# Branch B's first projection chunk among the attention fillers, and a three-piece end for the last tile's normalization

## The chip, the core and the metric

One core of a Trainium2 chip runs the kernel. Its engines each work through a queue of their own: TensorE (PE in the profile, its weight loads PEld), VectorE (DVE), ScalarE (ACT), GpSimd (POOL), and SyncE (SP), which issues the DMAs here. The metric is the device time of one execution in microseconds, lower is better; a kernel is executed several times and the median is given.

## What is computed

A single encoder layer on x of 1024 tokens by 1024 channels, float32:

```python
h = x @ w_in[l]
qa, ka, va, qb, kb, vb, ga, gb = jnp.split(h, split_pts, axis=-1)
y_a = chunk_band_attention(heads_a(qa), heads_a(ka), heads_a(va), rel_bias[l]) @ w_proj_a[l]
y_b = stick_breaking_attention(heads_b(qb), heads_b(kb), heads_b(vb)) @ w_proj_b[l]
gate_a = jax.nn.sigmoid(ga + b_gate[l, :D])
gate_b = jax.nn.sigmoid(gb + b_gate[l, D:])
mix = (gate_a * y_a + gate_b * y_b) @ w_out[l]
x = layer_norm(DEEPNORM_ALPHA * x + mix, ln1_g[l], ln1_b[l])
...
x = layer_norm(DEEPNORM_ALPHA * x + ffn, ln2_g[l], ln2_b[l])
```

There are 8 heads of width 64 in each branch. Branch A is softmax attention over a band with a bias by distance; branch B weights keys by a product of sigmoids over the keys between. The feed-forward block between the two normalizations is a gated one with 2816 hidden channels.

## The kernel before

**Numbers.** Every float32 operand is split into a high and a low part, and a product is three matmuls (high by high, high by low, low by high) into one accumulator in PSUM. A matmul is 128 by 128 weights against up to 512 columns.

**Stages.** The input projection comes first (to about 333 us of the span), with seven products for eight. Then attention (333 to 638 us), then branch B's projection with its gates (638 to 682 us), the output projection and the first normalization, and the feed-forward block, whose last part adds four hidden blocks to each of eight row tiles, normalizes the tile and stores it.

**Attention and its fillers.** The loop over `vsteps` (from L1021) takes 16 heads in turn, branch A's eight first, each in 12 steps. `hidx` is the head and `pos` the step in it. A step issues some score blocks ahead of need (`wunits`, as many as `LEAD` says), one group of transposes (`turn`) and, two steps late, the products with v (`mult`). A score block gives work to DVE, ScalarE and GpSimd, and the transposes wait for it. To fill PE in the meantime there is a generator, `fill_all` (L871), of independent matmuls of 512 columns: six gate chunks of 48 matmuls (tile `gps`), then branch A's projection, eight chunks of 24 (tile `yAps`), 480 in all. `goal` counts how many should have been issued; `fill_until(t)` issues up to `t`. `FILL[hidx]` is added to `goal` over a head's 12 steps, `AHEAD = 8` at the very start, and a few steps move it by hand: head 7, the last of branch A, is given 2 at step 3 and 4 at step 4, so that PE has something to do while the next branch starts. Whatever is left is issued after the last step.

**Order.** The framework that builds the program sorts instructions by their place in the text and by when they should be ready; what `tc.keep_in_program_order` names keeps its order. `turn(tied)` names its first transpose so. Each engine then runs its own queue in order, and an instruction that waits holds up those behind it.

**Buffers.** Tiles are taken from rings of buffers by tag (`SLOTS`, and `BANKS` for PSUM: two accumulators each of "mm" and "sc", three of "tr", one of "pv"). A new tile waits until the old one in its buffer has no user left. Fillers use "mm", scores use "sc", transposes "tr".

**Branch B's projection** (the loop at L1128) goes over eight chunks of 128 output channels in the order 6, 7, 5, 4, 2, 3, 1, 0. Each has two halves of 512 tokens, and a half is four operand tiles `yh[4 + k]`, `yl[4 + k]` (one for each pair of heads) times three matmuls: 12. Half 0 accumulates in an "sc" bank, half 1 in an "mm" bank (tile `yBps`). DVE multiplies each by the gate (L1146) and adds branch A's part (L1147); then the sums for the output projection follow, on ScalarE and DVE. The weights of two chunks come as one pair of tiles, `begin_proj(1, cc)`, the first of them at step 4 of the last head. After chunk 6 the weights of the output projection are split (`end_21()`, tile `wl_o` at L552).

**The last tile.** `layer_norm` (L1177) gathers statistics on DVE, raises the variance to a power on GpSimd, and then DVE does `(t - mean) * g`. With `quick` set, DVE also does `t * scale + b`, for each piece in `cuts` (L1190), and `done` stores the piece. Without it, ScalarE scales the whole tile (L1194) and GpSimd adds b (L1195). Of the eight tiles at the end only the last has `quick`, with two pieces of 512.

Of the kernel before, what the change touches and what calls it, by code (L numbers as in the profile page):

```python
# [13 lines left out]
AF = mybir.ActivationFunctionType  # L14
ALU = mybir.AluOpType
# [3 lines left out]
P = 128  # L19
S = 1024  # L20
D = 1024
# [9 lines left out]
HW = 512  # L31
LO, HI = slice(0, HW), slice(HW, 2 * HW)
# [3 lines left out]
LAG = 2  # L36
LEAD = ((6, 8, 9, 9, 10, 10, 11, 11, 12, 12, 13, 13), (7, 8, 9, 9, 10, 10, 11, 11, 12, 12, 13, 14))

FILL = (18, 18, 18, 18, 18, 18, 18, 34, 39, 39, 38, 38, 39, 37, 38, 38)
AHEAD = 8  # L40


# [6 lines left out]
def hybrid_trunk_kernel(ctx: ExitStack, tc, x, xt, w_first, w_v, w_in, b_gate, rel_bias, w_proj,  # L49
# [6 lines left out]
    nc = tc.nc  # L56
# [19 lines left out]
    def bank(tag, name):  # L76
        return ps.tile([P, HW], F32, tag=tag, name=name, bufs=BANKS[tag])
# [4 lines left out]
    mm = nc.tensor.matmul  # L82
# [208 lines left out]
    for j in range(4):  # L291
        cs = (LO, HI)[j % 2]
# [578 lines left out]
    def fill_all():  # L871
# [23 lines left out]
        for cc in range(4):  # L895
# [29 lines left out]
            if cc < 3:  # L925
                w = got.pop()

    def begin_proj(br, cc):

        hl = [slot("op", f"wy{p}{br}_{cc}", F32R) for p in "hl"]  # L930
        for d, t in zip(wp_dr[4 * br + cc], hl):
            dma(t.bitcast(F32), d)
        return lambda: hl
# [87 lines left out]
    for si, (hd, g, st, box) in enumerate(vsteps):  # L1021
        hidx, pos = si // nhead, si % nhead
        if hidx < 14 and pos == 8:
            load_qk(heads[hidx + 2])
            if hidx < 6:
                later.append([3, heads[hidx + 2]["end_bias"]])
        if pos == 4:
            if hidx < 15:
                load_v(heads[hidx + 1])
            else:  # L1030
                next_w = begin_proj(1, 3)()
                end_11, end_21 = (begin_wo(name, raws, "xt")
                                  for name, raws in (("11", ("qs", "kh")), ("21", ("kl", "v"))))
        if hidx == 15 and pos == 10:
            end_11()
        early = hd["br"] == 0 and st == LAG - 1 and len(pend) == LAG
        if early and g == 1:
            pend.pop(0)()
        if hidx == 7 and pos in (3, 4):
            if pos == 4:  # L1040
                fill_until(goal + 2)
            goal += pos - 1 + pos // 4
        elif hd["br"] == 0 and pos in (3, 5):
            goal += 4 - pos
        if hd["br"] == 0 and pos == 2:
            fill_until(goal + 0.5)
        tied = False
        while wi < min(hidx * 8 + LEAD[hd["br"]][pos], len(wunits)):
            wunits[wi]()
            wi += 1  # L1050
            tied = hd["br"] == 1
        if hidx == 7 and pos == 4:
            tied = True
            fill_until(goal)
        elif tied:
            fill_until(goal + 1)
        if si == 0:
            goal += AHEAD
            heads[1]["end_bias"](False)
            fill_until(goal)  # L1060
        if st == 0:
            steps_of[(hidx, g)] = value_steps(hd, g, box)
        turn, mult = steps_of[(hidx, g)][st]
        for item in list(later):
            item[0] -= 1
            if item[0] == 0:
                later.remove(item)
                item[1]()
        turn(tied)
        last = goal  # L1070
        goal += FILL[hidx] / nhead
        fill_until(0.5 * (last + goal))
        if early and g == 0:
            pend.pop(0)()
        pend.append(mult)
        wait = hd["br"] == 0 and st == LAG
        while len(pend) > LAG + wait:
            pend.pop(0)()
        fill_until(goal)
# [48 lines left out]
    for n, c in enumerate((6, 7, 5, 4, 2, 3, 1, 0)):  # L1128
# [7 lines left out]
        if c in kept:  # L1136
            mA = kept[c]
        else:
            mA = slot("op", f"mA{c}")
            dma(mA, m_dr[c])  # L1140
        for hf, cs in enumerate((LO, HI)):
            acc = bank(("sc", "mm")[hf], f"yBps{c}_{hf}")
            mm3(acc, [(w[0][:, ks], w[1][:, ks], yh[4 + k][:, cs], yl[4 + k][:, cs])
                      for k, ks in ((k, slice((c % 2) * HW + k * P, (c % 2) * HW + (k + 1) * P))
                                    for k in range(4))])
            nc.vector.tensor_tensor(gB[:, cs], acc, gB[:, cs], ALU.mult)  # L1146
            nc.vector.tensor_tensor(mA[:, cs], gB[:, cs], mA[:, cs], ALU.add)  # L1147
        m_raw[c] = mA
# [28 lines left out]
    def layer_norm(t, g, b, name, quick, done=lambda cs: None, n_st=2, cuts=(LO, HI)):  # L1177
# [8 lines left out]
        nc.gpsimd.tensor_tensor(mv[:, 2:3], mv[:, 1:2], neghalf, ALU.pow)  # L1186
        nc.vector.scalar_tensor_tensor(t, t, mv[:, 0:1], g, ALU.subtract, ALU.mult)
        if quick:
            for cs in cuts:
                nc.vector.scalar_tensor_tensor(t[:, cs], t[:, cs], mv[:, 2:3], b[:, cs],  # L1190
                                               ALU.mult, ALU.add)
                done(cs)
        else:
            nc.scalar.activation(t, t, AF.Copy, scale=mv[:, 2:3])  # L1194
            nc.gpsimd.tensor_tensor(t, t, b, ALU.add)  # L1195
            done(slice(0, D))
# [362 lines left out]
    for tt in range(8):  # L1559
        end = tt == 7  # L1560
        down_plain(last, tt, add_to, ((0, HW), (HW, 768), (768, D)) if end else ((0, HW), (HW, D)))
        layer_norm(acc_t[tt], *norm2, f"2_{tt}", end,
                   lambda cs: dma(out[tt * P:(tt + 1) * P, cs], acc_t[tt][:, cs]),
                   4 if end else 2)


def granules(w):
# [39 lines left out]
```

## Time and profile before

| | |
|---|---|
| median of 3 runs | 1420.0 us (1419.78 to 1420.16) |
| the profiled execution | 1420.21 us |
| its span | 1418.4 us |
| PE, PEld, DVE, ACT, POOL busy | 99%, 83%, 74%, 48%, 17% |
| granted TensorE clock, mean | 0.999 |
| DMA | 276.54 MB, mean 195 GB/s |

The profile is one execution of the program on the chip. Its span goes from the first to the last instruction that counts; the execution's own time has 1.8 us around it. "Busy" sums the durations of an engine's instructions. Matmuls overlap and their ends are modelled, so PE's pace is read from start to start. In a view in order of time a row is start, duration, engine, line, operation, tiles out<-in, shapes, how many were merged, and in brackets how long the engine was idle before it and what ended that. In the chain of waits a row is start, duration, engine and line. In a view by windows each engine has its busy time and its count of instructions, and the last three numbers are the granted clock, the DMA engines' share and GB/s. In a view of waits a row ends with the total, the number of times and the longest.

### The profile page before, as it was taken

What the parts mean: (1) busy time and instruction counts of PE and PEld (TensorE: products, weight loads), DVE (VectorE), ACT (ScalarE), POOL (GpSimd) and SP (SyncE); (2) the same over time, 40 slices, a digit from 0 to 9 for tenths busy, and PEclk for the clock granted to TensorE, in tenths of its full rate; (3) what the DMA queues carried; (4) which work ended last, traced back from release to release, by engine and by line L of the source; (5) the groups of instructions that cost most, each with busy time, mean ns of one, the idle gap of its engine ahead of it and who ended that gap; (6) DMA issues with size and microseconds to landing.
All of it is one profiled execution on the core that took longest, in us unless ns stands there. A gap on an engine that the chain in (4) does not pass through costs nothing.

```text
span 1418.4 us, 19023 instructions
## 1 busy us (share of the span) xinstructions
PE 1408.0 (99%) x6672; PEld 1171.7 (83%) x6672; DVE 1054.1 (74%) x1669; ACT 684.7 (48%) x1193; POOL 246.5 (17%) x318
## 2 busy tenths in 40 slices
PE   9999999999999999999999999999999999999997
PEld 7888888888888888888888888888888888888886
DVE  8967657535887778878998947777676656978757
ACT  6544444555888887874424624444344433212201
POOL 0000000002656888840001000000000000100014
PEclk9999999999999999999999999999999999999999
DMA  7486468846676469656651214444334458787502
GB/s 253 163 291 223 169 250 306 293 180 220 220 234 191 148 235 304 242 178 219 228 191 60 89 60 163 157 148 156 135 147 164 159 182 288 278 314 238 202 15 104
DMA packets 104974, 276.54 MB, mean 195 GB/s; under 512 B 10400, under 2 KB 26784, under 8 KB 104880
## 3 DMA queue, kind: packets, MB, share of 16 engines
q1 hardware_dynamic: 104880, 275.35, 55.4%
q8 instruction: 52, 0.85, 0.2%
q14 instruction: 42, 0.34, 0.1%
HBM read 179.33 MB, written 92.30 MB: 192 GB/s over the span
## 4 chain that ended last, share of the span: by engine, by line
PE 91%; DVE 2%; DMA 2%; ACT 1%; issue 1%; POOL 1%; SPq 0%; DVEq 0%; POOLq 0%; ACTq 0%
PE sxf L180 16%; PE sxp L180 9%; PE szf L180 8%; PE dx L1529 6%; PE v L482 5%; PE szp L180 4%; PE syf L180 4%; PE gps L607 4%; PE dz L1529 3%; PE ops L1375 3%; PE yAps L911 3%; PE syp L180 2%; PE tp_a L818 2%; PE tp_b L818 2%; PE fpswh_h L118 2%; PE fpswh_h L117 2%
## 5 line engine op out<-in xcount | busy, mean ns | idle before, releaser
L1485 POOL TENSOR_TENSOR wdyt<-wdyt 128x512 f32<-128x512 f32 x8 | 11.2, 1404 | 512.8 <-DMA sd<-s_dr 443.6
L795 POOL TENSOR_TENSOR w_b<-w_b,kp_b 128x511 f32<-128x511 f32 (+3 forms) x96 | 96.1, 1014 | 23.5 <-DVE kp_b L790 17.0
L790 DVE TENSOR_TENSOR_SCAN kp_b<-kp_b,ident_ps 128x512 f32<-128x512 f32 (+2 forms) x64 | 56.5, 885 | 21.2 <-ACT kp_b L787 20.3
L787 ACT ACTIVATE kp_b<-sc_b 128x512 f32<-128x512 f32 (+3 forms) x96 | 48.1, 501 | 28.0 <-PE sc_b L707 20.9
L180 PE MATMUL szf<-x1S63h,wcf 128*128 128x512 f32 x168 | 55.1, 389 | 0.0
L111 DVE TENSOR_TENSOR pt_b<-tp_b,pt_b 128x512 fp32r<-128x512 f32 (+1 forms) x96 | 49.9, 544 | 6.6 <-ACT pt_b L110 5.7
L730 POOL MEMSET bias<- 64x64 f32 x2 | 0.3, 144 | 313.7 <-ACT bias L726 313.7
L1460 DVE TENSOR_TENSOR x<-dx,x 128x512 f32<-128x512 f32 x64 | 43.4, 686 | 14.9 <-PE dx L1529 14.9
L111 DVE TENSOR_TENSOR sl<-h,sl 128x512 fp32r<-128x512 f32 x56 | 38.4, 686 | 20.5 <-ACT sl L110 20.5
L110 ACT CAST sl<-h 128x512 fp32r<-128x512 f32 x56 | 34.7, 619 | 36.9 <-PE syf L180 17.1
L760 POOL TENSOR_SCALAR w_a<-w_a,st_a 128x640 f32<-128x640 f32 (+2 forms) x64 | 42.2, 667 | 50.4 <-PE sc_a L707 27.0
L110 ACT CAST pt_b<-tp_b 128x512 fp32r<-128x512 f32 (+1 forms) x96 | 46.6, 502 | 8.2 <-PE tp_b L818 8.0
L1186 POOL TENSOR_TENSOR mv<-mv,neghalf 128x1 f32<-128x1 f32 x16 | 12.2, 760 | 220.6 <-DVE mv L1185 220.5
L1306 ACT ACTIVATE h<-sxf 128x512 f32<-128x512 f32 x21 | 12.6, 598 | 77.0 <-PE sxf L180 77.0
L755 ACT ACTIVATE w_a<-w_a,st_a 128x640 f32<-128x640 f32 (+2 forms) x64 | 44.7, 699 | 8.6 <-DVE st_a L749 7.5
L788 ACT ACTIVATE w_b<-sc_b 128x511 f32<-128x511 f32 (+3 forms) x96 | 48.2, 502 | 0.0
L818 PE MATMUL tp_b<-ident,w_b 128*128 128x128 f32 x288 | 47.3, 272 | 0.4 <-DVE pt_b L111 0.2
L111 DVE TENSOR_TENSOR pt_a<-tp_a,pt_a 128x512 fp32r<-128x512 f32 (+1 forms) x96 | 44.6, 485 | 3.3 <-ACT pt_a L110 2.2
L818 PEld LDWEIGHTS tp_b<-ident,w_b 128*128 128x128 f32 x288 | 36.4, 140 | 11.3 <-DVE pt_b L111 1.3
L110 ACT CAST pt_a<-tp_a 128x512 fp32r<-128x512 f32 (+1 forms) x96 | 39.3, 430 | 11.5 <-PE tp_a L818 10.6
L818 PE MATMUL tp_a<-ident,w_a 128*128 128x128 f32 x240 | 42.9, 275 | 0.4 <-DVE pt_a L111 0.3
L607 PE MATMUL gps<-xl,wh_g 128*128 128x512 f32 x96 | 41.7, 434 | 0.0
(1789 smaller groups left out, 4815.2 us busy)
## 6 DMA issues: line engine op xcount, KB each, us to landing
s_dr<-sl SPq DMA_DIRECT2D x112, 256.0 KB, 2.3
sd<-s_dr SPq DMA_DIRECT2D x56, 512.0 KB, 4.9
wLf<-in_w_ffn_in_dram SPq DMA_DIRECT2D x22, 512.0 KB, 4.3
wRf<-in_w_ffn_in_dram SPq DMA_DIRECT2D x22, 512.0 KB, 3.6
v_dr<-vc SPq DMA_DIRECT2D x16, 512.0 KB, 3.2
qs<-q_dr SPq DMA_DIRECT2D x16, 512.0 KB, 6.6
kh<-k_dr SPq DMA_DIRECT2D x16, 512.0 KB, 5.7
kl<-k_dr SPq DMA_DIRECT2D x16, 512.0 KB, 7.1
```

The source lines that it names most:

```text
L110: return (nc.scalar.copy(dst_h, src), nc.vector.tensor_tensor(dst_l, src, dst_h.bitcast(F32), ALU.subtract))
L111: nc.vector.tensor_tensor(dst_l, src, dst_h.bitcast(F32), ALU.subtract))
L180: mm(acc, lw[:, ks], rx, start=(first and kt == i == 0), stop=(kt == 3 and i == 2), skip_group_check=not first)
L482: mm(accs[j], a, b, start=(first and kt == n == 0), stop=(kt == 3 and n == 2), skip_group_check=True)
L607: mm(acc[hf], lw[:, ks], rx[k][:, (LO, HI)[hf]], start=(k == j == 0), stop=(k == KT - 1 and j == 2))
L755: nc.scalar.activation(s[:, 0:w], s[:, 0:w], AF.Exp, bias=st[:, m:m + 1], scale=-1.0, accum_out=st[:, 2:3])
L787: nc.scalar.activation(kp[:, c0:e], sc[:, 0:n], AF.Sigmoid, scale=-1.0)
L788: nc.scalar.activation(be[:, m0:e], sc[:, m0 - c0:n], AF.Sigmoid)
L790: nc.vector.tensor_tensor_scan(kp[:, 0:e], kp[:, 0:e], ident_ps()[:, 0:e], 0.0, ALU.mult, ALU.add)
L795: nc.gpsimd.tensor_tensor(be[:, m0:e], be[:, m0:e], kp[:, m0 - 1:e - 1], ALU.mult)
L818: ins = tr(tp[:, (qb - lo_q) * P:(qb - lo_q + 1) * P], wt[qb - q0][:, (kb - qb) * P:(kb - qb + 1) * P], ident)
L1529: mm(acc, a, b, start=(first and i == n == 0), stop=(i == n - 1 == 1), skip_group_check=not first)
```

## The change

Three matmul groups of each half (k = 0 to 2, so the first three pairs of heads) of branch B's chunk 6, 18 matmuls, become the last of the fillers. `part_b` is a new generator that issues any of a chunk's groups; `accs_b` keeps the accumulators between calls. The weights are asked for at step 10 of head 14 instead of step 4 of head 15. The goals rise by 18: 4 each at steps 1 and 2 of head 0, 2 at step 5 of head 7, and 1 in each of heads 8 to 15. At steps 1 and 2 of head 0 half of the four go ahead of the score blocks and the rest ahead of the transposes, which are tied there; so are head 7's at step 5.

In the projection loop chunk 7's first three groups of both halves (18 matmuls) are issued ahead of chunk 6's last group; then chunks 6 and 7 take their last group, and the other chunks are as they were.

In the last tile's normalization the second piece of 512 becomes two of 256. DVE does the first of them as it did; for the second, ScalarE scales and GpSimd adds b. Each piece is stored by itself, so that there are three stores.

```diff
-FILL = (18, 18, 18, 18, 18, 18, 18, 34, 39, 39, 38, 38, 39, 37, 38, 38)
+FILL = (18, 18, 18, 18, 18, 18, 18, 34, 40, 40, 39, 39, 40, 38, 39, 39)
...
+        for hf in range(2):
+            for _ in part_b(6, hf, state["w"], range(3)):
+                yield 1.0
+
+    accs_b = {}
+
+    def part_b(c, hf, w, kts):
+        if (c, hf) not in accs_b:
+            accs_b[c, hf] = bank(("sc", "mm")[hf], f"yBps{c}_{hf}")
+        cs = (LO, HI)[hf]
+        for k in kts:
+            ks = slice((c % 2) * HW + k * P, (c % 2) * HW + (k + 1) * P)
+            for n, (lw, rx) in enumerate(((w[0], yh), (w[0], yl), (w[1], yh))):
+                mm(accs_b[c, hf], lw[:, ks], rx[4 + k][:, cs], start=(k == n == 0),
+                   stop=(k == 3 and n == 2))
+                yield
...
+        if hidx == 14 and pos == 10:
+            state["w"] = next_w = begin_proj(1, 3)()
...
-                next_w = begin_proj(1, 3)()
...
-        if hd["br"] == 0 and pos == 2:
+        first = hidx == 0 and pos in (1, 2)
+        if first:
+            goal += 4
+            fill_until(goal - 2)
+        elif hidx == 7 and pos == 5:
+            goal += 2
+        elif hd["br"] == 0 and pos == 2:
             fill_until(goal + 0.5)
...
-        if hidx == 7 and pos == 4:
+        if first or (hidx == 7 and pos in (4, 5)):
             tied = True
             fill_until(goal)
...
+        if n == 0:
+            for hf in range(2):
+                for _ in part_b(7, hf, w, range(3)):
+                    pass
         for hf, cs in enumerate((LO, HI)):
-            acc = bank(("sc", "mm")[hf], f"yBps{c}_{hf}")
-            mm3(acc, [(w[0][:, ks], w[1][:, ks], yh[4 + k][:, cs], yl[4 + k][:, cs])
-                      for k, ks in ((k, slice((c % 2) * HW + k * P, (c % 2) * HW + (k + 1) * P))
-                                    for k in range(4))])
+            for _ in part_b(c, hf, w, range(3 if n < 2 else 0, 4)):
+                pass
+            acc = accs_b.pop((c, hf))
...
-            for cs in cuts:
-                nc.vector.scalar_tensor_tensor(t[:, cs], t[:, cs], mv[:, 2:3], b[:, cs],
-                                               ALU.mult, ALU.add)
+            for n, cs in enumerate(cuts):
+                if n < 2:
+                    nc.vector.scalar_tensor_tensor(t[:, cs], t[:, cs], mv[:, 2:3], b[:, cs],
+                                                   ALU.mult, ALU.add)
+                else:
+                    nc.scalar.activation(t[:, cs], t[:, cs], AF.Copy, scale=mv[:, 2:3])
+                    nc.gpsimd.tensor_tensor(t[:, cs], t[:, cs], b[:, cs], ALU.add)
                 done(cs)
...
-                   4 if end else 2)
+                   *((4, (LO, slice(HW, 768), slice(768, D))) if end else ()))
```

## The prediction

> **What bounds the kernel now.** I read the page, then the busy time by stage, then the chain of waits and the order of time inside attention.
>
> ```profile
> PE 1408.0 (99%) x6672; PEld 1171.7 (83%) x6672; DVE 1054.1 (74%) x1669; ACT 684.7 (48%) x1193; POOL 246.5 (17%) x318
> core 0: us, PE busy (x) PEld busy (x) DVE busy (x) ACT busy (x) POOL busy (x), PEclk, DMA share, GB/s
> 333.30:638.20 304.90, 303.62 (x1777) 259.08 (x1776) 246.85 (x578) 247.10 (x595) 204.99 (x276) 1.00 0.66 215
> 638.20:681.70 43.50, 43.50 (x195) 35.99 (x194) 38.56 (x67) 20.33 (x34) 0.00 (x0) 1.00 0.57 206
> 681.70:714.00 32.30, 32.30 (x144) 26.77 (x143) 28.86 (x43) 13.98 (x16) 0.12 (x1) 1.00 0.75 264
> 975.58 2.72 PE sxf L180 x12
> L117 PE MATMUL yBps<-yh,wyh x64: 389/389/447, 638.2 to 681.2; 128*128 128x512 f32 x64
> ```
>
> PE (TensorE's matmuls) is busy for 99% of the span, so only waits of PE can be won. The three windows are attention with its fillers (333.3 to 638.2), branch B's projection, and the start of the output projection. A row says 389 ns for a matmul of 512 columns, but twelve of them take 2.72 us in the chain: the pace is 0.227 us, and the 389 ns overlap the next one. Branch B's projection is 3 x 64 = 192 such matmuls in 43.5 us, again 0.227 us each: **no wait at all**. So what leaves that stage for attention saves 0.227 us a piece there, and costs the same in attention unless PE was waiting there. The gain is the wait that gets covered and nothing else. The overlap also hides waits: the busy time of a gap is short by 0.39 - 0.227 = 0.16 us, so I read waits from start to start.
>
> **The eight matmuls put into head 0.** The chain of waits, and PE in order of time:
>
> ```profile
> 334.12 2.97 DMA g_dr<-c
> 337.16 4.94 DMA kl<-k_dr
> 342.14 0.41 PE sc_a L707
> 338.71 0.39 PE L607 MATMUL gps<-xh,wh_g 128*128 128x512 f32 x1
> 339.23 0.33 PE L818 MATMUL tp_a<-ident,w_a 128*128 128x128 f32 x1
> ...
> 341.24 0.41 PE L706 MATMUL sc_a<-kh,qs 128*128 128x320 f32 x1
> 341.62 0.44 PE L818 MATMUL tp_a<-ident,w_a 128*128 128x128 f32 x2
> 342.14 0.41 PE L707 MATMUL sc_a<-kl,qs 128*128 128x320 f32 x1
> ```
>
> Head 1's low key tile sits in a buffer of the stage before. Its load is issued when the store g_dr<-c has landed (337.16) and lands 4.94 us later; at 342.14 the second score matmul of head 1's first block starts. From 341.24 to 342.14 are 0.90 us; the work in it is 320 columns (0.227 x 320/512 = 0.14) and two transposes (0.44 less the 0.33 of the last is 0.11 each): 0.36. **Lost: 0.54 us.** From 338.71 to 339.23 a 0.227 us matmul is followed by 0.29 us of waiting for the first softmax weights. Together 0.83 us.
> In the kernel's text the changed goals put 17 fillers instead of 12 ahead of that block, and 19 instead of 12 ahead of the turn behind it. The load's time hangs on the store, not on PE, so 5 x 0.227 = 1.13 us of work goes in ahead of a moment that does not move. Bounds 0.83 and 1.13 us; as there are smaller waits between, I take **1.0 us**. Scores that now stand behind two fillers come 0.45 us later; behind them wait DVE's maxima and the softmax of ScalarE, both 81% busy over the whole stage by the window above, so with room to make it up.
>
> **The two at the change from branch A to B (head 7, step 5).**
>
> ```profile
> 454.46 0.39 PE L607 MATMUL gps<-xl,wh_g 128*128 128x512 f32 x1
> 455.12 0.66 PE L818 MATMUL tp_a<-ident,w_a 128*128 128x128 f32 x4 [0.28 <-DVE pt_a L111]
> ```
>
> 0.66 us from start to start, 0.227 of it work: 0.43 us lost, waiting for DVE to free a transpose bank. Two fillers are 0.45 us, tied ahead of a turn here. If they land behind the gap the gain is 0; I take **0.4 us**, since step 5 is where it lies.
>
> **The eight spread over heads 8 to 15.**
>
> ```profile
> 540.56 0.39 PE L911 MATMUL yAps<-yh,wyl 128*128 128x512 f32 x1
> 541.10 0.42 PEld L818 LDWEIGHTS tp_b<-ident,w_b 128*128 128x128 f32 x4 [0.58 <-DVE pt_b L111]
> PEld tp_b L818 <- DVE pt_b L111: 1.3, 3, 0.6
> PEld tp_b L818 <- PE sc_b L707: 0.9, 2, 0.5
> PEld pv_b L833 <- DVE yt L841: 0.7, 3, 0.4
> PEld gps L607 <- ACT gate L612: 0.3, 1, 0.3
> ```
>
> The last four are all waits of the weight loads from 470 to 638: 3.2 us in 9 places. A load runs ahead of its matmul, so its wait overstates the loss: at 541.10 it waited 0.58 us and PE lost 0.54 - 0.227 = 0.31. At that ratio (0.53) the nine cost 1.7 us. One filler more per head is 8 x 0.227 = 1.81 us, but it falls on one step of twelve and the waits sit in a few. Bounds: 0 (none meets a wait) and 1.7; I take **0.7 us**, nearer the lower, since the goals are spread evenly and the waits are not. The last 18 fillers are now branch B's own for chunk 6. They need yh and yl of pairs 4 to 6, split a head earlier, and one "sc" bank that scores no longer use; their weights come by two loads whose place moves up six steps on SP's queue, past the load of a head's v.
>
> ```profile
> 567.88 0.38 SPq L932 DMA_DIRECT2D wyh<-wp_dr  x1
> 577.98 0.32 SPq L932 DMA_DIRECT2D wyl<-wp_dr  x1
> ```
>
> These are the fifth of eight such pairs, so branch B's first, and were issued 60 us before 638.2 already; I price the move at nothing. Were that cover gone, it would be a load's 4.9 us (the key tile's above).
>
> **Behind attention.** Now chunk 7's first 18 matmuls run first, then the 3 that are left of each half of 6 and of 7. The last pair's operand was first read by the 10th matmul (low half) and the 22nd (high half), now by the 19th and again the 22nd, so no wait grows there. But four accumulators finish within 12 matmuls (2.72 us) instead of 48, and DVE empties them.
>
> ```profile
> 643.44 0.69 DVE L1146 TENSOR_TENSOR gB<-yBps,gB 128x512 f32<-128x512 f32 x1 [0.36 <-ACT gB L961]
> ...
> 648.04 2.36 DVE L552 TENSOR_TENSOR wl_o<-wr_o,wh_o 128x1024 fp32r<-128x1024 f32 x2 [0.26 <-ACT wh_o L551]
> 650.32 1.28 DVE L1146 TENSOR_TENSOR gB<-yBps,gB 128x512 f32<-128x512 f32 x2
> ...
> 682.11 0.68 DVE L1146 TENSOR_TENSOR gB<-yBps,gB 128x512 f32<-128x512 f32 x1
> ```
>
> From its first product of chunk 6 to the first of chunk 7 DVE takes 650.32 - 643.44 = 6.88 us. Counted from the stage's first matmul: chunk 6's first half is complete after 21 matmuls (4.76 us), allowing DVE 0.2 us to see it (chosen), it starts at 4.96, reaches chunk 7 at 11.84 and has freed the first of its banks at 12.48 (half of 1.28). Chunk 4's first half wants that bank after 18 + 12 + 24 = 54 matmuls, at 12.24: about **0.3 us** of new waiting. It is 0 if the 2.36 us of weight splits go behind, and 0.7 if DVE's own small waits double. DVE then runs behind PE, and has 43.5 - 38.56 = 4.9 us idle in the stage to catch up.
>
> **The last tile.**
>
> ```profile
> 1408.66 1.15 ACT L1194 ACTIVATE x<-x,mv 128x1024 f32<-128x1024 f32 x1 [4.29 <-DVE x L1187]
> ...
> 1413.78 1.41 DVE L1190 SCALAR_TENSOR_TENSOR x<-x,mv,ln2b 128x512 f32<-128x512 f32 x2
> L1195 POOL TENSOR_TENSOR x<-x,ln2b x7: 2374/2402/2407, 1377.2 to 1409.9; 128x1024 f32<-128x1024 f32 x7
> L1563 SPq DMA_DIRECT2D out_dram<-x x9: 332/332/338, 1379.6 to 1415.2; - x9
> out_dram<-x SPq DMA_DIRECT2D x4, 512.0 KB, 2.6
> out_dram<-x SPq DMA_DIRECT2D x2, 256.0 KB, 2.0
> 1415.35:1416.80 1.45, 0.00 (x0) 0.00 (x0) 0.00 (x0) 0.00 (x0) 0.00 (x0) 0.59 0.97 360
> ```
>
> DVE writes two halves from 1413.78 and SP sends each. New: DVE half and quarter, ScalarE and GpSimd the last quarter beside them. By columns ScalarE needs at least 1.15/4 = 0.3 us and GpSimd 0.6, so that quarter is ready by 1414.8 or so, DVE's by 1414.9; DVE's second half was ready at 1413.78 + 1.41 = 1415.19. But SP takes 0.33 us for each store: the first still waits for the first half (about 1414.5), the third then goes no sooner than 1415.2, where the last one of two goes now. And from 1415.35 the DMA engines are 97% busy at 360 GB/s, 1.45 us, which is all of the 512 KB: the stores run end to end, so a shorter last one ends no earlier. Taken **0**; a store of 128 KB by itself would land in 2.0 - 0.3 = 1.7 us (the two rows give 0.6 us for 256 KB), so up to 0.3 us gained; twice as many packets or a late GpSimd, 0.2 lost. The Trainium skill ("DMA: Bandwidth & Descriptors", "Anatomy of one DMA") prices each DMA of the GpSimd path at about 2.0 us plus its bytes over 436 GB/s; carried over to SP, the tail would gain 0.3 us, and the sum would be 0.3 lower. The trace has stores that queue behind each other, which that price leaves out.
>
> **The sum.** 1.0 + 0.4 + 0.7 = 2.1 gained, 0.3 lost: -1.8 us. The profiled execution took 1420.21 us (1418.4 span and 1.8 around it), so 1418.4; it stood 0.2 above the median of 1420.0, so I forecast **1418.2 us**.
>
> **The rivals.**
> Every added filler meets a wait: 1.13 + 0.45 + 1.7 = 3.3 gained, no wait behind attention: 1416.7. For it, DVE, ScalarE and GpSimd are all busy for 67 to 81% of attention and PE waits where they bunch. Against it, the even spread.
> Attention has no room: the 18 matmuls cost there the 4.1 us that they save, and the 0.3 stays: 1420.3. For it, PE's 303.62 of 304.90 us; against it, the four gaps above, and that the key tile's load does not move. The Trainium skill ("Perfetto Trace Analysis", "Identifying the Most-Contended Engine") says that a matmul row's busy time misleads and that the share of weight loads tells how near PE is to its limit. By that rule attention (259.08 of 304.90, 85%) is fuller than the projection (35.99 of 43.50, 83%), which runs without a wait, and this rival would hold; the trace disagrees, for transposes load weights as often for a quarter of the columns.
> **Slower:** DVE becomes the bound behind attention. It began the stage's products 643.44 - 638.2 = 5.2 us after PE, now 4.96, but with 4.08 us of matmuls less to come: 3.8 us of lag by the stage's end if none of its idle time can be used. The last accumulator was emptied by 682.8, and its bank is wanted 12 matmuls after 681.7, at 684.4: 1.6 us of lag are free, the rest, 2.2, PE waits. With 0.3 lost and only the two first gains (1.4) it gives 1421.1. With those gains it turns the sign from 2.7 us of lag on. For it, DVE is 89% busy there (38.56 of 43.5) and still at 28.86 of 32.30 behind it; against it, the 4.9 us of idle time, most of it before 665.
>
> **How the numbers follow.** Forecast 0.48; all covered 0.25; no room 0.12; DVE behind 0.15. I call 0.2% (2.84 us) what a measurement tells from no change, so faster means under 1417.16, slower over 1422.84. Faster: most of the second case (0.21) and the lower end of the first (0.09): 0.30. Slower: DVE's case where its lag costs 2 us more than priced, and what I have not thought of: 0.10. Same: 0.60. The range goes from half a microsecond under the all-covered case, for the tail's 0.3 and a free bank, to the slower case's price: 1416.1 to 1421.1.
>
> **What would show it.** Right: the second score matmul of head 1 still starts near 342.1, with five more fillers before it and no wait of half a microsecond; the gap at 454.5 is gone; attention is about 2 us longer by the start of the stage behind it, not 4; one wait of some 0.3 us at chunk 4's first half; the third store of the last tile is issued as long after DVE's start on it as the second is now (1415.2 against 1413.78), and lands no sooner after. Wrong: a load of keys or weights that lands late in head 0, waits in heads 8 to 15 that stay or grow, DVE emptying the last accumulators over 1.6 us after PE, or a re-sorted order with new gaps in attention.

## The result, and the profile after

| | before | after |
|---|---|---|
| median of 16 runs each, on one chip | 1420.08 us (1419.40 to 1421.48) | 1422.42 us (1422.06 to 1423.61) |
| the profiled execution, and its span | 1420.21, 1418.4 us | 1422.20, 1420.2 us |

The ratio is 1.0016 (1.0009 to 1.0022): the change makes the kernel **2.3 us slower**. 1418.2 us was forecast, and the time lies above the range, which ended at 1421.1. The ratios, here and below, leave out two executions that took 1660 and 1753 us. From the page after:

```profile
PE 1407.9 (99%) x6672; PEld 1171.6 (82%) x6672; DVE 1054.4 (74%) x1669; ACT 685.0 (48%) x1194; POOL 247.6 (17%) x319
```

The work is the same to a tenth of a microsecond, so the 1.8 us between the two spans are waits. Three matmuls divide the span: attention's first score, the output projection's first matmul, and the last matmul of all. Before, then after, PE in order of time:

```profile
333.31 0.30 PE L706 MATMUL sc_a<-kh,qs 128*128 128x320 f32 x1
...
681.87 0.39 PE L1375 MATMUL ops<-wh_o,m 128*128 128x512 f32 x1
...
1410.77 0.28 PE L120 MATMUL fpswh_h<-wh_fo,wl_h 128*128 128x256 f32 x1
```

```profile
332.93 0.30 PE L706 MATMUL sc_a<-kh,qs 128*128 128x320 f32 x1
...
683.27 0.39 PE L1406 MATMUL ops<-wh_o,m 128*128 128x512 f32 x1
...
1412.15 0.28 PE L120 MATMUL fpswh_h<-wh_fo,wl_h 128*128 128x256 f32 x1
```

Attention with branch B's projection holds the same matmuls in both kernels. It took 348.56 us and now takes 350.34: **1.78 us more**. From there to the last matmul both take 728.9 us. From the last matmul to the span's end it was 7.6 us and is 8.0: **0.4 us more**. (Attention began 0.4 us earlier in this execution; its start moved by up to 2.3 us between the executions below, 332.4 to 334.7 us.)

**Where attention waits now.** The stretch of 346 to 452 us lies in heads 1 to 7. Its row in the busy time by windows, before and after:

```profile
346.00:452.00 106.00, 105.94 (x667) 93.00 (x666) 83.86 (x313) 88.44 (x225) 61.15 (x78) 1.00 0.65 201
```

```profile
346.00:452.00 106.00, 104.78 (x662) 92.20 (x661) 84.00 (x314) 86.60 (x224) 60.61 (x77) 1.00 0.66 197
```

PE had hardly a gap there (0.06 us); now 1.22 us of it are idle, although ScalarE is no busier than it was. The first gap, and the same place before, in order of time:

```profile
348.32 0.56 ACT L612 COPY gate<-gps 128x512 f32<-128x512 f32 x1
...
348.78 0.62 ACT L551 CAST wh_g<-wr_g 128x512 fp32r<-128x512 f32 x1
...
349.31 0.75 ACT L110 CAST pt_a<-tp_a 128x384 fp32r<-128x384 f32 x2
...
349.95 0.34 PE L833 MATMUL pv_a<-pt_a,v 128*128 128x384 f32 x1
...
350.04 0.89 DVE L111 TENSOR_TENSOR pt_a<-tp_a,pt_a 128x384 fp32r<-128x384 f32 x2
...
350.65 0.45 PE L834 MATMUL pv_a<-pt_a,v 128*128 128x384 f32 x1 [0.37 <-DVE pt_a L111]
```

```profile
347.43 0.96 ACT L110 CAST pt_a<-tp_a 128x384 fp32r<-128x384 f32 x2
...
348.00 0.56 DVE L111 TENSOR_TENSOR pt_a<-tp_a,pt_a 128x384 fp32r<-128x384 f32 x1
...
349.04 0.34 PE L833 MATMUL pv_a<-pt_a,v 128*128 128x384 f32 x1
...
349.22 0.33 PE L834 MATMUL pv_a<-pt_a,v 128*128 128x384 f32 x1
```

Between the two matmuls PE needs 0.17 us for 384 columns; it takes 0.18 before and 0.70 after. What PE waits for goes from the transposes through ScalarE's cast (L110) to DVE's subtraction (L111). Before, the cast began 1.6 us ahead of the first of the two matmuls. Now it stands on ScalarE behind the copy of a finished half of a gate (L612) and the cast of half of the next gate's weights (L551), and begins 0.64 us ahead. Both belong to the fillers: each gate chunk of 48 brings two copies, two casts on ScalarE and two subtractions on GpSimd. At 390.4 (0.46 us lost) the gate's copy and cast stand on ScalarE, busy without a break from 388.2 on, ahead of the copy that empties the accumulator of the products with v (L852). At 433 it is the cast of the transposes again; between the rows shown ScalarE is busy without a break:

```profile
431.05 0.60 ACT L612 COPY gate<-gps 128x512 f32<-128x512 f32 x1
431.53 0.64 ACT L551 CAST wh_g<-wr_g 128x512 fp32r<-128x512 f32 x1
...
433.39 1.03 ACT L110 CAST pt_a<-tp_a 128x256 fp32r<-128x256 f32 x3
...
432.94 0.48 PE L607 MATMUL gps<-xl,wh_g 128*128 128x512 f32 x1
433.82 0.39 PE L833 MATMUL pv_a<-pt_a,v 128*128 128x256 f32 x1 [0.40 <-ACT pt_a L110]
```

Another new gap lies in head 11, where GpSimd writes two low halves of branch A's operand (2.53 us together) ahead of the stick-breaking weights for which a transpose waits:

```profile
534.11 2.53 POOL L972 TENSOR_TENSOR yl<-yraw,yh 128x512 fp32r<-128x512 f32 x2
536.60 0.86 POOL L795 TENSOR_TENSOR w_b<-w_b,kp_b 128x319 f32<-128x319 f32 x1
...
536.03 0.49 PE L818 MATMUL tp_b<-ident,w_b 128*128 128x128 f32 x3
537.52 0.33 PE L818 MATMUL tp_b<-ident,w_b 128*128 128x128 f32 x1 [1.00 <-POOL w_b L780]
```

### The profile page after: what moved, and what is told of

The parts are those of the page before. It is cut to its first block, busy times and chain, and to the rows that moved or that the text cites. A ratio compares the mean times of both kernels' runs of the same rounds, so it can differ in the third digit from the quotient of the medians.

```text
span 1420.2 us, 19025 instructions
## 1 busy us (share of the span) xinstructions
PE 1407.9 (99%) x6672; PEld 1171.6 (82%) x6672; DVE 1054.4 (74%) x1669; ACT 685.0 (48%) x1194; POOL 247.6 (17%) x319
## 4 chain that ended last, share of the span: by engine, by line
PE 94%; DVE 2%; ACT 1%; issue 1%; DMA 1%; POOL 0%; DVEq 0%; ACTq 0%; POOLq 0%
PE sxf L180 16%; PE sxp L180 9%; PE szf L180 8%; PE dx L1560 6%; PE v L482 5%; PE gps L607 4%; PE szp L180 4%; PE syf L180 4%; PE yBps L941 3%; PE dz L1560 3%; PE yAps L911 3%; PE ops L1406 3%; PE syp L180 2%; PE tp_b L818 2%; PE tp_a L818 2%; PE plain L348 2%
## 5 line engine op out<-in xcount | busy, mean ns | idle before, releaser
L111 DVE TENSOR_TENSOR pt_b<-tp_b,pt_b 128x512 fp32r<-128x512 f32 (+1 forms) x96 | 50.1, 544 | 11.2 <-ACT pt_b L110 10.3
L111 DVE TENSOR_TENSOR sl<-h,sl 128x512 fp32r<-128x512 f32 x56 | 38.4, 686 | 21.2 <-ACT sl L110 21.2
L110 ACT CAST sl<-h 128x512 fp32r<-128x512 f32 x56 | 34.7, 619 | 37.5 <-PE syf L180 17.1
L110 ACT CAST pt_b<-tp_b 128x512 fp32r<-128x512 f32 (+1 forms) x96 | 46.8, 501 | 11.0 <-PE tp_b L818 10.4
L111 DVE TENSOR_TENSOR pt_a<-tp_a,pt_a 128x512 fp32r<-128x512 f32 (+1 forms) x96 | 44.7, 486 | 4.1 <-ACT pt_a L110 2.7
L110 ACT CAST pt_a<-tp_a 128x512 fp32r<-128x512 f32 (+1 forms) x96 | 39.0, 429 | 15.1 <-PE tp_a L818 14.0
```

The source lines that it names most:

```text
L110: return (nc.scalar.copy(dst_h, src), nc.vector.tensor_tensor(dst_l, src, dst_h.bitcast(F32), ALU.subtract))
L111: nc.vector.tensor_tensor(dst_l, src, dst_h.bitcast(F32), ALU.subtract))
```

## The experiments

Each run's time is the median of 11 runs; the ratio is to the kernel before in runs between them on the same chip (medians 1419.80 to 1420.16 us). The intervals are about 1.2 us to either side, so the traces decide between neighbours. "Extra" is worked out from the starts on PE: the time from attention's first score to the output projection's first matmul, less that of the run without any additional goal (e4, 348.11 us: 332.79 to 680.90). The kernel before has 0.45 on this scale and the changed kernel 2.2. "Extra by" some place compares the start of the same matmul in both, less 0.227 us for each filler more that stands before it.

Four executions share the order of the kernel before through attention: its own, e1, e12 and e4, with 0.45, 0.00, -0.19 and 0.00 extra. So 0.6 us between two executions can be chance. By the end of head 7 the last three agree within 0.05 us, and the kernel before stands 0.35 above them, all of it since its late key tile.

### The change in its parts

The changed last tile alone, on the kernel before (e1), and everything but the last tile (e2):

```diff
 # the last tile undone (e2), in all the runs below marked "old tail"
-                   *((4, (LO, slice(HW, 768), slice(768, D))) if end else ()))
+                   4 if end else 2)
```

> The kernel before with the new end of the last tile alone. Theory (GpSimd's addition slows the VectorE piece that runs beside it: 945 ns for 256 columns in the changed kernel's profile against about 430 for such a piece, so the last two stores go out later): the time from VectorE's first scaled piece to the end grows from 4.6 to about 5.0 us, and the kernel is 0.4 us slower than before. Rival (the end is bound by the stores and neutral, as forecast; the 0.4 us is the scatter of one profile): the same within 0.1 us, and the piece takes about 430 ns.

> The changed kernel with the old end of the last tile. Theory: 0.4 us faster than the changed kernel, so 1.9 us slower than before. Rival (the end is neutral): as slow as the changed kernel, 2.3 us over before. Both: the order in attention is the changed kernel's, and its waits stay where they were.

Without head 0's eight fillers (e3, shown; the step's condition is never true), and without any of the eighteen additional goals (e4):

```diff
-        first = hidx == 0 and pos in (1, 2)
+        first = False
```

> The changed kernel without the eight fillers of head 0 (they come after the last step instead). Theory (running the filler stream 8 ahead shifts what the stream itself asks of ScalarE, VectorE and GpSimd against the heads' steps, and new waits come up in heads 1 to 6): the 1.1 us of waits that branch A's heads gained are gone, and the kernel is 0.5 to 1.2 us slower than before. Rival (the fillers of heads 8 to 15 and the projection loop cost it, not head 0): 2 us or more slower than before.

> The changed kernel with all goals as before: the 18 matmuls of chunk 6 come after the last step, then chunk 7's, and the new end of the last tile stays. The order in attention is that of the kernel before. Theory: the end costs 0.4 us and the new order of chunks 6 and 7 at most 0.3, so 0.4 to 0.7 us slower than before. Rival (VectorE falls behind after attention, as the slower case of the forecast had it): 1.5 us or more slower than before.

Only half of head 0's fillers, and only the eight of heads 8 to 15, both with the old tail:

```diff
 # e7
-            goal += 4
-            fill_until(goal - 2)
+            goal += 2
+            fill_until(goal - 1)
```

> The changed kernel with the old end and four fillers in head 0 instead of eight. Theory (alignment): where the waits fall depends on the shift; heads 1 to 6 have waits at other places, and the cost isn't half. Rival (each filler put into head 0 costs its share): the cost over the version without head 0's fillers is half of that of eight, 1.0 to 1.3 us.

> Of the changed goals only the eight in heads 8 to 15, with the old end and the new order of chunks 6 and 7. Theory (the spread fillers do meet waits, 0.5 us in all by the trace without head 0's eight, and the end costs 0.35): 0.4 to 0.6 us faster than before, the best of all so far. Rival (that gain came from the two of head 7, or is scatter of one profile): as before within 0.2 us.

| run | median us | ratio | extra us |
|---|---|---|---|
| e1, tail alone | 1419.92 | 0.9999 (0.9990 to 1.0008) | |
| e2, all but the tail | 1421.93 | 1.0012 (1.0003 to 1.0021) | 2.09 |
| e3, all but head 0's eight | 1419.66 | 0.9999 (0.9991 to 1.0008) | -0.54 |
| e4, no additional goals | 1420.01 | 1.0003 (0.9994 to 1.0012) | 0 |
| e7, four in head 0, old tail | 1421.80 | 1.0014 (1.0005 to 1.0023) | 2.14 |
| e8, heads 8 to 15 alone, old tail | 1419.73 | 1.0000 (0.9991 to 1.0009) | 0.43 |

**Head 0's eight fillers carry the loss**: what holds them here is 2 us slower, what leaves them out is as fast as the kernel before. The price isn't one for each filler, since four cost as much as eight, and the four cost it at other places: e7 has only 0.3 us extra by the start of head 7, then loses 0.53 us where a score matmul of branch B waits for ScalarE (`w_b`, at 455.5) and 0.67 in head 11. So what follows on heads 1 to 6 holds for the displacement by eight. The new projection order (in e3 and e4) and the eight of heads 8 to 15 cost nothing that can be told, and gain nothing: the 0.4 to 0.6 us of e8's theory did not come. e3's attention is the shortest of all, but 0.5 us less in one execution lies inside the scatter, and its time doesn't tell it from nothing. e1 has the tail of the changed kernel, 8.0 us from the last matmul to the end; its time can't show the 0.4 us either.

e4 has the order of the kernel before through attention, and shows how much of the key tile's wait, on which head 0's gain rested, belonged to one execution:

```profile
340.72 0.41 PE L706 MATMUL sc_a<-kh,qs 128*128 128x320 f32 x1
341.09 0.44 PE L818 MATMUL tp_a<-ident,w_a 128*128 128x128 f32 x2
341.28 0.39 PE L707 MATMUL sc_a<-kl,qs 128*128 128x320 f32 x1
```

From 340.72 to 341.28 are 0.56 us with the same 0.36 of work: 0.2 us lost, where the profile of before had 0.54. e1 and e12 agree with e4 up to here within 0.05 us.

### Place or displacement?

Eight fillers in head 0 also move all later fillers: up to head 7 each comes eight fillers early against the heads, and so does what the gates ask of ScalarE and GpSimd. First attempt, with the displacement taken back in head 1 (old tail):

```diff
-FILL = (18, 18, 18, 18, 18, 18, 18, 34, 40, 40, 39, 39, 40, 38, 39, 39)
+FILL = (18, 10, 18, 18, 18, 18, 18, 34, 40, 40, 39, 39, 40, 38, 39, 39)
```

> The changed kernel with the old end, and head 1 given 10 fillers instead of 18: the eight of head 0 are taken back there, so from head 2 on the filler stream stands to the heads as in the kernel without head 0's eight. Theory (the shift of the stream against the heads makes the later waits): the waits of heads 3 to 6 (1.1 us) are gone and so is what they pass on; 0.5 us that heads 0 and 1 cost stays; about 1.5 us faster than with the shift, within 0.5 us of before. Rival (a shuffled order makes waits anywhere, whatever the alignment): still 1.5 us or more over before.

1421.92 us, 1.0016 (1.0007 to 1.0025): nothing came back. But 1.5 of the 2.05 us extra are lost by head 2, with waits of 0.53, 0.27 and 0.25 us at 351 to 361 us: head 1 has only ten fillers left, so its own waits lie open. The run took cover away and can't decide. Next, eight fillers put ahead of all of attention's turns, and the opposite, each on e8:

```diff
-AHEAD = 8
+AHEAD = 16    # e13; 0 in e14
```

> Head 0's eight additional fillers are not put in at its steps 1 and 2, but ahead of all of attention's turns (16 there instead of 8); the rest is as in the run in which only heads 8 to 15 have their additional filler (1419.7 us), with the old last tile. From head 1 to head 6 the built order of the matmuls is then that of the changed kernel, but none of the eight is tied or stands at the late key tile. Theory A (displacement: the gates' own work on ScalarE, VectorE and GpSimd stands eight fillers earlier against the heads until head 7, and meets other steps there): as slow as the changed kernel with the old last tile, 1421.5 to 1422.2 us, with the waits of 0.3 to 0.6 us near 350, 390 and 427 us. Rival B (the place: the tied fillers at steps 1 and 2 hold up the scores behind them): as before, 1419.5 to 1420.2 us.

> The same with the displacement the other way: no filler ahead of attention's turns instead of 8, so that the gates' work stands eight fillers later against the heads until head 7, with nothing else moved against the run with heads 8 to 15 alone (1419.7 us). Theory A (any displacement breaks the fit that heads 0 to 7 have now): 1 to 2.5 us slower, with new waits in heads 0 to 7, though not at the places of the changed kernel. Rival B (only an earlier boundary of the gates does harm, because it falls on the steps with four transposes): 1419.3 to 1420.2 us.

e13 took 1421.44 us, 1.0012 (1.0002 to 1.0021), 1.43 us extra, against e8's 0.43. None of its additional fillers stands at head 0's scores or is tied, and it has the waits of the changed kernel at 390.8 (0.47 us), 427.6 (0.32) and 433.4 (0.55), and 0.31 of the one at 350. By the end of head 7 it has 1.0 us extra, e2 1.4. **So in heads 1 to 7 it is the displacement, for the most part, and not the place.** It doesn't account for all of the loss: e2's other 0.7 us lie behind, and e13 lacks the wait of head 11. That wait stands in the changed kernel, e2, e6 and e7, which have fillers in head 0 and head 7's two, and not in e3, e5 (which takes head 0's back), e8 or e13; no run separates its cause.

e14 took 1421.77 us, 1.0011 (1.0002 to 1.0020), 1.91 extra: 0.9 of it by the end of head 1, which it leaves without cover, and 0.9 in head 7, with the same 0.53 us wait for ScalarE as in e7. So the other direction is no better, though partly for the reason of e5.

### What is displaced

The gate-weight splits later in each chunk, on the changed kernel with the old tail (e6) and on e8 (e17). This is e6's edit, nine fillers later for both halves of a split:

```diff
                 if hf:
                     acc.append(bank("mm", f"gps{i}_1"))
-                    half_way()
                 for k in range(KT):
+                    if hf and k == 3:
+                        half_way()
                     yield from part(hf, k)
-                    if hf and k == 2 and rest:
+                    if hf and k == 5 and rest:
                         rest.pop()()
```

In e17 the two `half_way` lines stand behind `yield from part(hf, k)`, so that the first half of a split comes 12 fillers later, not nine as its expectation says; the second comes nine later.

> The changed kernel with the old end, and the splits of the next gate's weights issued 9 fillers later in each gate chunk, which puts them back about where they stood against the heads. Theory (of the stream's own work it is these splits on ScalarE and GpSimd that now collide with the heads): the waits of heads 3 to 6 fall from 1.1 us to under 0.4, 0.7 us or more faster than the changed kernel with the old end. Rival (the gate copies or the order as a whole): no more than 0.2 us faster, other waits in place of these.

> The run with only heads 8 to 15's additional filler (1419.7 us), with the gate-weight splits nine fillers later, as in the run that made the displaced kernel 1.2 us faster. Theory A (a matter of fit: the splits' place suits the heads as they stand in the kernel before, and any move against them costs): 0.5 to 1.5 us slower, 1420.2 to 1421.2. Rival B (later splits are better wherever the fillers stand): as fast or faster, 1418.7 to 1419.7.

e6: 1420.73 us, 1.0008 (0.9999 to 1.0017), 0.96 us extra where e2 has 2.09. The waits at 350, 390 and 433 us are gone and the one at 427 stays (0.33 us); two others (0.60 and 0.22 us) come at 405 and 416. So the time fell as the theory had it, but the rival's other waits came too. e17: 1420.31 us, 1.0002 (0.9993 to 1.0011), 0.32 extra where e8 has 0.43, and no idle PE from 346 to 452 us: on undisplaced fillers a like edit changes nothing that can be told. Its time lies at the lower end of theory A's range, but 0.15 us from the kernel before on its chip. Later isn't better everywhere, and that every move of the splits costs is not shown.

The decisive pair leaves the splits out. The next gate's weights are replaced by tiles that were split earlier, two loads in place of one; TensorE's instructions stay. On e8 (e15) and on e13 (e16):

```diff
-            end = begin_gate(i + 1, nc.gpsimd)
-            yield from gate(i, w, lambda: got.append(end(True, rest)))
+            end = begin_proj(*divmod(i % 8, 4))
+            yield from gate(i, w, lambda: got.append(end()))
```

> The run with only heads 8 to 15's additional filler (1419.7 us), without the splitting of the five gate weights that are split among the fillers: in place of each, two tiles that were split and stored earlier (those of the projections) are loaded, so ScalarE's casts and GpSimd's subtractions for them fall away and the gates are not the reference's; TensorE's instructions stay as they are. It is the undisplaced half of a pair. Both theories: not slower than 1419.7; the waits that the splits cause in it fall away, 1418.7 to 1419.7 us.

> The same without the splits, with the eight fillers ahead of attention (16 instead of 8): the displaced half of the pair, which stood at 1421.4 against 1419.7 with the splits. Theory A (the gates' splits on ScalarE and GpSimd, displaced against the heads, make the new waits): at most 0.5 us slower than its pair without displacement. Rival B (the order of TensorE's own instructions after the displacement, or the gates' copies and loads, make them): again 1.3 to 2.0 us slower than its pair, with waits near 350, 390 and 427 us.

| | not displaced | eight ahead | medians' difference |
|---|---|---|---|
| with splits | e8 1419.73 | e13 1421.44 | 1.7 us |
| without | e15 1419.30, 0.9997 (0.9988 to 1.0005) | e16 1419.76, 1.0001 (0.9992 to 1.0010) | 0.5 us |

Only differences along a row count: e15 and e16 also end 0.3 us sooner after the last matmul (7.35 us, e8 and e13 7.67), for a reason that no run shows. The 0.5 us lies inside the intervals.

The window of heads 1 to 7 in e8, e13, e15 and e16:

```profile
346.00:452.00 106.00, 105.94 (x666) 93.08 (x665) 83.77 (x314) 88.44 (x226) 60.68 (x78) 1.00 0.66 204
```

```profile
346.00:452.00 106.00, 105.02 (x664) 92.44 (x664) 84.12 (x316) 87.05 (x225) 60.32 (x76) 1.00 0.64 202
```

```profile
346.00:452.00 106.00, 106.00 (x666) 93.07 (x665) 84.15 (x317) 86.57 (x221) 53.84 (x72) 1.00 0.70 218
```

```profile
346.00:452.00 106.00, 106.00 (x672) 93.53 (x671) 84.83 (x318) 86.13 (x221) 53.65 (x72) 1.00 0.73 226
```

The displacement costs 0.92 us of idle PE with the splits and nothing without, although the loads that stand in for the splits keep the DMA engines busier (0.73 against 0.64). The place of the first gap in e13, then in e16, shows why:

```profile
348.90 0.56 ACT L612 COPY gate<-gps 128x512 f32<-128x512 f32 x1
349.37 0.62 ACT L551 CAST wh_g<-wr_g 128x512 fp32r<-128x512 f32 x1
349.89 0.75 ACT L110 CAST pt_a<-tp_a 128x384 fp32r<-128x384 f32 x2
```

```profile
348.62 0.56 ACT L612 COPY gate<-gps 128x512 f32<-128x512 f32 x1
349.09 0.75 ACT L110 CAST pt_a<-tp_a 128x384 fp32r<-128x384 f32 x2
```

The copy stands ahead of the cast in both; only the 0.62 us of the weights' cast is missing, and with it the wait. By the end of head 7, e13 has lost 1.0 us against e8, and e16 has gained 0.4 against e15, but only 0.1 against e8: the cover that the fillers were meant to give is somewhere between. e13 and e16 differ by 1.15 us there. In heads 8 to 15 the pair without splits then loses 0.7 us and the pair with them nothing; no cause was separated there.

The wait in head 11 was tried by itself: four of branch A's low halves on DVE instead of GpSimd, on e6.

```diff
-            nc.gpsimd.tensor_tensor(lo, raw[:, cs], hi.bitcast(F32), ALU.subtract))
+            (nc.vector if i < 4 and cs is HI else nc.gpsimd).tensor_tensor(
+                lo, raw[:, cs], hi.bitcast(F32), ALU.subtract))
```

> The changed kernel with the old last tile, the gate-weight splits nine fillers later, and now the low half of four y splits (pairs 0 to 3, second half of the columns) on VectorE instead of GpSimd. It stands against the run with later splits alone, 1420.7 us. Theory A (the 0.92 us wait of head 11's transposes near 535.5 us comes from GpSimd, which is held by two y splits of 2.5 us each while the weights of the transposes wait behind them): that wait is gone, the time falls by 0.7 to 0.9, to about 1419.9. Rival B (VectorE, 81% busy over the stage, is as short as GpSimd: the splits of some 0.7 us each delay its own casts of the transposes): the wait moves to VectorE, the time stays at 1420.5 to 1421.0.

1422.88 us, 1.0018 (1.0009 to 1.0028), 2.0 us extra where e6 has 0.96: slower than either expectation. GpSimd's wait is gone, but DVE's four subtractions, expected at 0.7 us each, took 0.68, 1.78, 0.68 and 1.16, and two waits of 0.98 and 1.04 us for DVE came in its place:

```profile
529.30 0.66 PE L819 MATMUL tp_b<-ident,w_b 128*128 128x128 f32 x4 [0.81 <-DVE pt_b L111]
...
533.48 0.44 PE L819 MATMUL tp_b<-ident,w_b 128*128 128x128 f32 x2 [0.87 <-DVE pt_b L111]
```

### The last tile

The changed tail on the kernel before, with the last quarter's offset on DVE:

```diff
-                    nc.gpsimd.tensor_tensor(t[:, cs], t[:, cs], b[:, cs], ALU.add)
+                    nc.vector.tensor_tensor(t[:, cs], t[:, cs], b[:, cs], ALU.add)
                 done(cs)
```

> The kernel before with the changed last tile, but the last 256 columns are offset by VectorE instead of GpSimd (ScalarE still scales them). Theory A (VectorE's second piece of 256 columns took 0.94 us because GpSimd's addition ran beside it): that piece takes 0.35 to 0.45 us, VectorE's addition another 0.3 to 0.4, and from the last matmul's start to the end are 7.6 to 7.7 us as in the kernel before, 0.3 less than with GpSimd. Rival B (the piece is slow for its own reason, its cut or its operands): it takes 0.9 us again and the tail 8.0 us. The time alone (1419.6 to 1420.1) will hardly tell.

1419.90 us, 0.9999 (0.9990 to 1.0008). The changed kernel, then e12, in order of time:

```profile
1415.17 1.61 DVE L1218 SCALAR_TENSOR_TENSOR x<-x,mv,ln2b 128x512 f32<-128x512 f32 x2
1415.74 0.75 POOL L1222 TENSOR_TENSOR x<-x,ln2b 128x256 f32<-128x256 f32 x1 [1.40 <-ACT x L1221]
```

```profile
1413.51 1.15 DVE L1191 SCALAR_TENSOR_TENSOR x<-x,mv,ln2b 128x512 f32<-128x512 f32 x2
1414.57 0.42 DVE L1195 TENSOR_TENSOR x<-x,ln2b 128x256 f32<-128x256 f32 x1
```

DVE's half and quarter take 1.61 us beside GpSimd, longer than the 1.41 us of two halves before, and 1.15 without it. From DVE's first piece to the span's end are 5.0 us after, 4.7 in e12 (span 1418.2), and 4.6 before. So the loss of the tail is GpSimd's addition beside DVE; the third store adds nothing that the rounding of the span lets see.

No run is faster than the kernel before by more than its interval.

## Why the prediction failed, step by step

**Head 0 (1.0 us gained).** This step turned the sign: "The gain is the wait that gets covered and nothing else", with the queues behind the moved work said to have "room to make it up" because DVE and ScalarE are 81% busy over the stage. The late key tile's wait is covered: five fillers more stand before head 1's second score, which starts without a wait.

```profile
342.44 0.31 PE L706 MATMUL sc_a<-kh,qs 128*128 128x320 f32 x1
342.59 0.31 PE L707 MATMUL sc_a<-kl,qs 128*128 128x320 f32 x1
```

It starts 0.45 us later than "near 342.1", though attention began 0.4 us earlier. Counted from attention's first score it comes 9.66 us in; it was 8.83 before, and is 8.49 in e4. The five fillers are 1.13 us of work, so they saved 0.3 us against the profile of before and nothing against e4. Two terms of the 1.0 us fail here. 0.34 of the 0.54 us came from one late load, which e1, e4 and e12 don't have. And the 0.29 us for the first softmax weights still stands, because the same ten fillers come ahead of it in both kernels, and all additional ones behind:

```profile
338.32 0.40 PE L607 MATMUL gps<-xh,wh_g 128*128 128x512 f32 x1
338.85 0.33 PE L818 MATMUL tp_a<-ident,w_a 128*128 128x128 f32 x1
```

What turned the sign is that the fillers were costed as matmuls alone. Their copies, casts and subtractions moved too, for seven heads, and met other steps: 0.6 us of casting ahead of an urgent cast makes a wait of 0.5. An average of 81% says nothing of the order in a queue. The prediction named "a re-sorted order with new gaps in attention" as what would make it wrong, and gave it neither a price nor a chance of its own.

**Head 7 (0.4 gained)** fell to nothing. The gap stands, at the same 0.66 us from start to start:

```profile
456.75 0.39 PE L607 MATMUL gps<-xh,wh_g 128*128 128x512 f32 x1
457.41 0.66 PE L818 MATMUL tp_a<-ident,w_a 128*128 128x128 f32 x4 [0.27 <-DVE pt_a L111]
```

The two fillers landed behind it. The gates' matmuls (`gps`) from attention's start up to that group of transposes, before and after, in a view by windows of that tile alone (PE, PEld and ScalarE):

```profile
333.30:455.00 121.70, 59.27 (x152) 27.09 (x152) 3.67 (x6) 1.00 0.66 205
```

```profile
332.90:457.30 124.40, 61.99 (x160) 28.41 (x160) 3.47 (x6) 1.00 0.68 202
```

Eight more stand ahead of the gap, and these are head 0's; head 7's two would make ten. They follow at once: from the gap to the second pair of products with v behind it (456.80 before, 459.64 after) there are five fillers instead of three. This is the case that the prediction gave no gain, "if they land behind the gap"; it took 0.4 us "since step 5 is where it lies". That reading was wrong. In the kernel's text a head's steps 0 to 5 have 4, 3, 2, 1, 4 and 3 transposes, 30 in all twelve, and those behind the gap are the 221st to 224th of branch A: step 4's. e3, which has head 7's two and not head 0's eight, shows the same: 152 fillers and a gap of 0.46 us.

**Heads 8 to 15 (0.7 gained)** gave nothing net: in e8 the wait of about 0.4 us at 506 is gone and one of 0.9 us at 541 has come. The lower bound, 0, was right. The 0.31 us that the prediction read at 541.10 belonged to one execution: e1, e4 and e12 have no wait there.

**Behind attention (0.3 lost)** was right in its mechanism and its size came out smaller.

```profile
643.65 0.45 PE L941 MATMUL yBps<-yh,wyh 128*128 128x512 f32 x1
...
648.76 1.30 DVE L1173 TENSOR_TENSOR gB<-yBps,gB 128x512 f32<-128x512 f32 x2 [1.18 <-PE yBps L941]
...
655.19 1.28 DVE L1173 TENSOR_TENSOR gB<-yBps,gB 128x512 f32<-128x512 f32 x2
...
655.97 0.45 PE L941 MATMUL yBps<-yh,wyh 128*128 128x512 f32 x1
...
684.86 0.68 DVE L1173 TENSOR_TENSOR gB<-yBps,gB 128x512 f32<-128x512 f32 x1
```

DVE's first product comes 5.1 us after the stage's first matmul (4.96 forecast) and chunk 7's 6.4 us later (6.88 forecast), so the bank is free at 655.8, just as PE wants it: under 0.1 us. At the end DVE lags by 2.3 us (684.86 + 0.68 - 683.27) instead of 0.9. That is 1.35 more than before, less than the 1.6 us that were free. The rival in which DVE becomes the bound fails here.

**The last tile (0)** lost 0.4 us, past its bound of 0.2: GpSimd's addition was priced by its columns, as running beside DVE for nothing.

**The rivals.** The slower one (1421.1) is nearest by its time, by luck: DVE behind attention, its mechanism, cost under 0.1 us. "No room" (1420.3) holds for the eight of heads 8 to 15, which gained nothing, but the waits that came are not in it, and e16 took eight fillers into heads 0 to 7 at no cost. All in all some 2 us in attention and 0.4 in the tail make the 2.3. On the scale of e4 the changed kernel has 1.25 us extra by the end of head 7 and 2.2 at the end. Of the former about 1 us is shown to come from the five gates' splits (1.0 to 1.5 by the pairs). The other 1.0, in heads 8 to 15, holds the wait of head 11, and its cause stays open.

## What to carry to other kernels

A filler isn't only a matmul: list what it brings along on the other engines, and look at the instructions that would stand right ahead of an urgent cast in the new order. Inserting work at one place in a tuned interleaving displaces all that follows; price that, or keep the displacement out. Count on which side of a gap the inserted work lands. A gap of half a microsecond in one execution is worth a second profile before anything is built on it.

## What was not expected of the hardware

A DVE instruction of 128x256 that reads two tiles took 0.94 us beside a GpSimd addition (the 1.61 us less the 0.67 from the first piece's start to the second's), and 0.48 in e12. DVE's second piece ends at 1416.78, and GpSimd's addition, which began some 0.1 us before that piece, at 1416.49: DVE seems to have stood still until GpSimd was done and then done its work in 0.29 us. In e1 the two ends are 0.28 us apart again. The Trainium skill ("SBUF — State Buffer", "SBUF: two separate sides") says that the two engines share a pair of ports as an exclusive lock, held for a whole instruction, also against a DVE instruction with two inputs in SBUF; these two traces agree with it, and by that rule the loss in the tail could have been forecast.
